# A two-block transformer kernel, rescheduled: new costs and a VectorE/GpSimd exclusion rule in the planner, a late softmax division, and a later write of the embedding

## The chip, the core and the metric

The kernel runs on one core of a Trainium2 chip. The metric is the device time of one execution in microseconds. Before the change it is 3984.7 us, the median of 3 runs (3984.07 to 3984.71).

## The reference, cut to what matters

Two blocks follow each other on 1024 positions of width 1024, all in float32.

- The first block has two layers. Each normalises `x` (and 256 context rows), scales and shifts it by a modulation computed from `c` (`silu(c) @ w_mod + b_mod`), projects it with `w_in`, runs two attentions of 6 heads and a convolution of 31 taps, gates the results and projects them with `w_out`.
- The second block has gated linear attention, a sparse attention of 16 heads over keys that an indexer picks (top 256), a mixing projection, a layer norm, a feed-forward net with a convolution of 3 taps, a layer norm, and a gated embedding (`sigmoid(x @ w_ple_gate) * (p @ w_ple)`) with a last layer norm.

The two places that the change rewrites are these:

```python
h = rms_norm(x, norm_w) * (1.0 + scale[:, None, :]) + shift[:, None, :]   # first layer, modulated input
...
logits = jnp.where(valid[:, :, None, :], logits, -jnp.inf)                # sparse attention
probs = jax.nn.softmax(logits, axis=-1).astype(kv_sel.dtype)
return jnp.einsum('bqhk,bqkc->bqhc', probs, kv_sel)
```

## The kernel before

Activations lie transposed, features on the 128 partitions, positions in chunks `c` of 512 (the context is a chunk of 256). A float32 product is made of three single-pass products: each operand is split into a rounded high part and the rest (`split`: a cast, then a subtraction, `lo`). So nearly every tile costs VectorE, ScalarE or GpSimd two instructions before TensorE may use it.

The program is first written as a list of operations with tags for the stages: `emb` (the products of the embedding), `nm0` (first norm), `mod0` (modulation), `cin0`, `in0`, `conv0`, `mla0`, `gqa0`, `out0` (first layer), the same with 1 (second layer), then `idx`, `score`, `topk`, `gla`, `glap`, `ckv`, `dsa` (sparse attention), `dsap`, `wo2`, `ffn` and `ple`. Each operation names the engines that may run it, with a cost for each (`alts`): sums and differences of two SBUF tiles may go to VectorE (`v`) or GpSimd (`p`), copies to ScalarE (`a`) or VectorE. `Plan.schedule` then walks through a modelled time, picks for each free engine the ready operation of the lowest rank (its place in the list plus `late`), and assigns buffers: 89 pages of 128x512 (`pg`), 8 PSUM banks (`ps`), some small tiles (`sm`). The order that it finds is the order in which each engine's instructions are emitted. So a changed cost changes the order, the engine and the buffers of instructions everywhere.

Every matrix product is recorded at one line (389), every transpose at 393, every sum of two tiles on VectorE at 330 and on GpSimd at 332, every scalar-tensor-tensor at 340, ScalarE's work at 289 and its scalings at 363, VectorE's scalings at 365 and 352. All DMAs are issued by SyncE (403).

In `dsa` a unit is a head and a chunk of 512 queries, four tiles of 128 queries. For each tile: scores (TensorE), masked maximum (line 1796, VectorE), exponentials with their sum (ScalarE), a reciprocal, and a scaling of the probabilities. Then the probabilities are transposed (TensorE), split, and multiplied with the values into the bank `acc`. 32 units run as a pipeline: the scores of the next unit are merged into the products of this one.

At the start `embed` makes 16 tiles in `emb`, and the function `put` (called `early` in `block1`) writes them to DRAM.

## Time and profile before

| | |
|---|---|
| median of 3 runs | 3984.7 us |
| profiled execution | 3984.33 us, of which its span 3982.5 us |
| TensorE busy | 3860.4 us (97%), 18344 matmuls |
| VectorE busy | 3130.6 us (79%) |
| ScalarE busy | 1964.9 us (49%) |
| GpSimd busy | 1520.0 us (38%) |
| mean granted TensorE clock | 0.99 |

TensorE is busy nearly all the time, so what can be had is in the 3%, in the stretches in which its clock is below full, and in what TensorE itself is given to do. A table by stretches of the span is the way to read it, since the idle time is not spread evenly.

### The profile page before, as it was taken

The page shows a single profiled execution, that of the slowest core. Times are in us where ns is not written, and L with a number is a line of the kernel's source. Part 1 is how long each engine was busy: PE and PEld are TensorE (multiplying, and loading weights), DVE is VectorE, ACT ScalarE, POOL GpSimd, SP SyncE. Part 2 cuts the span into 40 slices and gives each one's busy share as a digit, 9 for nine tenths or more (in the row PEclk, how much of TensorE's full clock was granted, in tenths as well). Part 3 has the DMA queues.
Part 4 walks back from the last instruction along what each step waited for, and adds up shares of the span by engine and source line. Part 5 has one row for each costly group of instructions (what it writes and reads, how often), then busy time and mean ns, then how long its engine had stood idle before and what let it go on. Part 6 is the DMA issues. An engine that isn't in the chain of part 4 may idle for free. (4 is left out here: it accounts for less than half of the span.)

```text
span 3982.5 us, 53245 instructions
## 1 busy us (share of the span) xinstructions
PE 3860.4 (97%) x18344; PEld 3100.5 (78%) x18344; DVE 3130.6 (79%) x5241; ACT 1964.9 (49%) x3841; POOL 1520.0 (38%) x1348
## 2 busy tenths in 40 slices
PE   6999999999999999999999999999999999999997
PEld 4778777768878777678988888877778788888876
DVE  8998899996796888857988985788776854446598
ACT  5345577763245566635355731566653432222255
POOL 7654465561252444522354531111143511111177
PEclk8999999999999999999999999999999999999998
DMA  7232222133232110232111332000054411111121
GB/s 247 82 119 79 63 68 65 47 115 135 69 121 72 31 30 20 87 116 73 57 55 60 126 111 77 29 29 34 25 191 127 146 42 49 51 51 43 49 86 57
DMA packets 184975, 311.82 MB, mean 78 GB/s; under 512 B 22912, under 2 KB 46208, under 8 KB 184704
## 3 DMA queue, kind: packets, MB, share of 16 engines
q1 hardware_dynamic: 184704, 308.42, 23.6%
q8 instruction: 144, 2.36, 0.2%
q14 instruction: 127, 1.04, 0.1%
HBM read 237.81 MB, written 62.39 MB: 75 GB/s over the span
## 5 line engine op out<-in xcount | busy, mean ns | idle before, releaser
L389 PE MATMUL ps<-pg,pg 128*128 128x512 f32 (+5 forms) x17008 | 3789.5, 384 | 43.6 <-ACT pg L289 19.8
L389 PEld LDWEIGHTS ps<-pg,pg 128*128 128x128 f32 (+3 forms) x17008 | 2955.4, 188 | 733.5 <-issue 72.9
L332 POOL TENSOR_TENSOR pg<-pg,pg 128x512 fp32r<-128x512 f32 (+4 forms) x1030 | 1437.2, 1411 | 2015.2 <-ACT pg L289 1037.8
L289 ACT ACTIVATE pg<-pg 128x512 fp32r<-128x512 f32 (+7 forms) x1385 | 785.7, 596 | 779.4 <-DVE pg L340 252.1
L289 ACT ACTIVATE pg<-ps 128x512 f32<-128x512 f32 (+10 forms) x1352 | 681.8, 551 | 870.3 <-PE ps L389 708.2
L330 DVE TENSOR_TENSOR pg<-pg,pg 128x512 fp32r<-128x512 f32 (+7 forms) x839 | 769.5, 930 | 150.9 <-ACT pg L289 99.2
L330 DVE TENSOR_TENSOR pg<-ps,pg 128x512 fp32r<-128x512 f32 (+9 forms) x650 | 367.5, 584 | 223.3 <-PE ps L389 133.9
L340 DVE SCALAR_TENSOR_TENSOR pg<-ux,c,pg 128x512 f32<-128x512 f32 x416 | 361.4, 895 | 22.5 <-ACT pg L289 13.9
L373 DVE TENSOR_REDUCE sm<-ps 128x1 f32<-128x512 f32 (+1 forms) x492 | 326.5, 681 | 26.8 <-PE ps L389 23.5
L298 DVE CAST pg<-pg 128x512 fp32r<-128x512 f32 (+4 forms) x342 | 210.9, 623 | 56.2 <-ACT pg L289 24.9
L340 DVE SCALAR_TENSOR_TENSOR pg<-pg,c,pg 128x512 f32<-128x512 f32 (+3 forms) x242 | 223.9, 962 | 5.6 <-ACT pg L289 4.9
L289 ACT ACTIVATE pg<-ps,c 128x512 f32<-128x512 f32 (+1 forms) x182 | 128.0, 708 | 202.9 <-PE ps L389 162.9
L393 PE MATMUL ps<-c,pg 128*128 128x128 f32 (+1 forms) x796 | 163.8, 272 | 11.4 <-DVE pg L298 6.0
L1541 DVE MAX8 sm<-ux 128x8 f32<-128x384 f32 (+5 forms) x192 | 166.9, 884 | 1.3
L1542 DVE MATCH_REPLACE8 ux<-sm,ux 128x384 f32<-128x384 f32 (+5 forms) x192 | 167.4, 875 | 0.0
L298 DVE COPY ux<-ps 128x512 f32<-128x512 f32 x79 | 54.5, 691 | 140.3 <-ACT pg L289 122.6
L389 PE MATMUL ps<-pg,c 128*128 128x512 f32 (+3 forms) x196 | 81.7, 482 | 54.8 <-DVE pg L330 21.7
L393 PEld LDWEIGHTS ps<-c,pg 128*128 128x128 f32 (+1 forms) x796 | 103.9, 141 | 37.9 <-DVE pg L298 6.0
L289 ACT ACTIVATE pg<-pg,sm 128x512 f32<-128x512 f32 (+2 forms) x192 | 116.3, 607 | 18.8 <-DVE sm L352 18.4
L678 ACT ACT_TABLE_LOAD x92 | 118.0, 1283 | 1.6
L383 POOL MEMSET pg<- 128x128 f32 (+2 forms) x193 | 49.9, 274 | 159.7 <-PE ps L389 99.0
L1796 DVE CUSTOM_DVE_ANT_0 pg<-ps,pg 128x512 f32<-128x512 f32 (+3 forms) x176 | 98.8, 573 | 11.6 <-PE ps L389 10.7
(73 smaller groups left out, 1024.7 us busy)
## 6 DMA issues: line engine op xcount, KB each, us to landing
d<-pg SPq DMA_DIRECT2D x202, 256.0 KB, 2.0
pg<-d SPq DMA_DIRECT2D x178, 256.0 KB, 3.5
pg<-in_w2a SPq DMA_DIRECT2D x108, 256.0 KB, 3.0
pg<-in_wmod SPq DMA_DIRECT2D x96, 256.0 KB, 3.3
pg<-in_wup SPq DMA_DIRECT2D x88, 256.0 KB, 2.7
pg<-in_win SPq DMA_DIRECT2D x80, 256.0 KB, 3.4
pg<-in_wout SPq DMA_DIRECT2D x64, 256.0 KB, 3.3
pg<-in_wdn SPq DMA_DIRECT2D x48, 256.0 KB, 2.7
```

The source lines that it names most:

```text
L289: nc.scalar.activation(real(out), real(in_), fn, scale=real(scale), **k)
L298: self.nc.vector.tensor_copy(real(out), real(in_))
L330: self.nc.vector.tensor_tensor(out=real(out), in0=real(in0), in1=real(in1), op=o)
L332: self.nc.gpsimd.tensor_tensor(out=real(out), in0=real(in0), in1=real(in1), op=o)
L340: self.nc.vector.scalar_tensor_tensor(out=real(out), in0=real(in0), scalar=real(scalar), in1=real(in1), op0=o0, op1=o1)
L373: lambda e: self.nc.vector.tensor_reduce(out=real(out), in_=real(in_), axis=AX.X, op=o))
L389: lambda e: self.nc.tensor.matmul(real(out), lhsT=real(lhsT), rhs=real(rhs), start=start, stop=stop))
L393: lambda e: self.nc.tensor.transpose(real(out), real(in_), real(ident)))
L678: nc.scalar.preload_act_table_set(pre)
L1541: P.vec(P.c_v(n), [w], [m8], lambda e, m8=m8, w=w: nc.vector.max(real(m8), real(w)))
L1542: P.vec(P.c_v(n), [w, m8], [w], lambda e, m8=m8, w=w: nc.vector.match_replace(real(w), real(m8), real(w), MARK))
L1796: lambda e, p=p, s=s, n=n, m=mk[t, b], a=sm[:, b:b + 1]: nc.vector.tensor_tensor_reduce(out=real(p), in0=real(s[:, 0:n]), in1=real(m), sca ...
```

## The change

**The planner's costs.** The fixed part of nearly every operation falls: VectorE's sums from 155 to 67 ns, its scalings from 190 to 110, GpSimd's sums from 200 to 92, ScalarE's work from 170 or 202 to 49 or 93. A result is then ready only `TAIL` after its engine is free.

**The exclusion.** Before, an operation on VectorE with SBUF inputs (`dual`) was planned up to 0.42 longer while GpSimd was busy. Now GpSimd's operations and VectorE's `dual` ones are planned one after the other, and GpSimd may take a sum only where VectorE could not have it done sooner.

**The start.** The 16 writes of the embedding (`early()`) are listed behind the modulated inputs. The scaling and shifting of these (`affine`) may go to ScalarE.

**The sparse attention.** The probabilities are no longer scaled. The reciprocals of the four tiles of a unit are transposed onto the feature axis by four transposes of a broadcast column (`rp`), copied to SBUF, and the output is multiplied by them, once for two heads. Maxima, their scaling and the reciprocals are made for four tiles at once; a second block of keys takes the first one's maximum as its start.

```diff
     def c_v(self, n, ex=0):
-        return (n * 1.04 + 155 + ex) / 1000
+        return (n * 1.04 + 67 + ex) / 1000
     def c_p(self, n):
-        return (n * 2.2 + 200) / 1000
+        return (n * 2.2 + 92) / 1000
...
+    def affine(self, out, in_, s, b):
+        def emit(e):
+            if e == "a":
+                self.nc.scalar.activation(real(out), real(in_), AF.Identity, bias=real(b), scale=real(s))
+            else:
+                self.nc.vector.tensor_scalar(out=real(out), in0=real(in_), scalar1=real(s), scalar2=real(b), op0=OP.mult, op1=OP.add)
+        return self.op({"v": (out.n * 0.52 + 110) / 1000, "a": self.c_act(out.n, in_, 93)}, [in_, s, b], [out], emit)
...
+        TAIL = {"t": 0.0, "a": 0.115, "v": 0.083, "p": 0.08, "d": 0.0}
+        hold = {"v": 0.0, "p": 0.0}
...
+                                elif e == "p" and m == "v":
+                                    apart = sum(x.alts["v"] for _, x in ready["v"][:6] if not issued[x.idx] and not x.dual)
+                                    if hold["v"] <= now:
+                                        apart += max(0.0, busy["v"] - now)
+                                    if len(ready["v"]) > 1 and apart + o.alts["v"] < o.alts["p"] + max(0.0, hold["v"] - now):
+                                        ok = False
...
-                    if e == "v" and o.dual and busy["p"] > now:
-                        c += 0.42 * min(busy["p"] - now, c / 0.58)
+                    if e == "p" or e == "v" and o.dual:
+                        other = "p" if e == "v" else "v"
+                        c += max(0.0, hold[other] - now)
+                        hold[e] = now + c
...
-        if c == 1:
-            early()
...
-            P.ts(t, t, a[:, i, k:k + 1].k(2 + k // 4), m[:, i, k:k + 1].k(k // 4), "mult", "add")
+            P.affine(t, t, a[:, i, k:k + 1].k(2 + k // 4), m[:, i, k:k + 1].k(k // 4))
...
+    early()
...
-                    P.ts(sm[:, 2:3], sm[:, 0:1], -(128.0 ** -0.5), None, "mult")
+                P.ts(sm[:, 0, :], sm[:, 0, :], -(128.0 ** -0.5), None, "mult")
...
-                    P.vec(0.08, [sm], [sm], lambda e, sm=sm: nc.vector.reciprocal(real(sm[:, 6:7]), real(sm[:, 4:5])))
-                    for b in range(nb):
-                        P.scale(pn[t, b], pn[t, b], sm[:, 6:7])
+                P.vec(0.2, [sm], [sm], lambda e, sm=sm: nc.vector.reciprocal(real(sm[:, 3, :]), real(sm[:, 1, :])))
...
+                rp = P.ps()
+                for t in range(4):
+                    P.tr(rp[0:64, t * 128:(t + 1) * 128], sm[:, 3, t:t + 1].to_broadcast([128, 64]), ident)
...
+                P.copy(rr[c][G, :].k(i), rp[0:64, :])
...
+                    P.tt(ob[c], ob[c], rr[c], "mult", "vp")
```

GpSimd's queue at the start of the program, before the change: the sums of squares of the first norm (written to one page, pg_220), then the low parts of the modulation weights, 128x512 each.

```order
L332 TENSOR_TENSOR pg_220<-pg_220,pg_227 128x512
L332 TENSOR_TENSOR pg_220<-pg_220,pg_249 128x512
L332 TENSOR_TENSOR pg_220<-pg_220,pg_266 128x512
L332 TENSOR_TENSOR pg_220<-pg_220,pg_276 128x512
L332 TENSOR_TENSOR pg_352<-pg_236,pg_337 128x512
L332 TENSOR_TENSOR pg_373<-pg_246,pg_346 128x512
L332 TENSOR_TENSOR pg_395<-pg_258,pg_377 128x512
L332 TENSOR_TENSOR pg_418<-pg_269,pg_397 128x512
```

The same place in the changed kernel (the sums of squares go to pg_215):

```order
L332 TENSOR_TENSOR pg_215<-pg_215,pg_229 128x512
L332 TENSOR_TENSOR pg_215<-pg_215,pg_256 128x512
L332 TENSOR_TENSOR pg_215<-pg_215,pg_263 128x512
L332 TENSOR_TENSOR pg_363<-pg_241,pg_337 128x512
L332 TENSOR_TENSOR pg_453<-pg_287,pg_416 128x512
L332 TENSOR_TENSOR pg_482<-pg_482,pg_507 128x512
L332 TENSOR_TENSOR pg_203<-pg_203,pg_518 128x512
L332 TENSOR_TENSOR pg_847<-pg_847,pg_853 128x256
```

Of GpSimd's low parts of the modulation weights two are left at this place; the others are now in VectorE's queue. Over the whole program GpSimd's queue goes from 1348 rows to 769, VectorE's from 4932 to 5069, TensorE's from 18083 to 18214.

VectorE's queue in the middle of `dsa` before the change (ISA is the masked maximum and the reading of its result, sm a tile's small numbers):

```order
L1796 ISA pg_26706,sm_26707<-ps_26676,pg_24863 128x512
L1796 ISA sm_26707 128x1
L1807 RECIPROCAL sm_26588<-sm_26588 128x1
L352 TENSOR_SCALAR sm_26660<-sm_26660 128x1
L365 TENSOR_SCALAR pg_26587<-pg_26587,sm_26588 128x128
L1796 ISA pg_26731,sm_26707<-ps_26691,pg_24877 128x128
L1796 ISA sm_26707 128x1
```

And in the changed kernel:

```order
L1824 ISA pg_26641,sm_26608<-ps_26616,pg_24941 128x512
L1824 ISA sm_26608 128x1
L298 COPY pg_26650<-ps_26469 64x512
L1824 ISA pg_26657,sm_26608<-ps_26627,pg_24968,sm_26608 128x384
L1824 ISA sm_26608 128x1
L330 TENSOR_TENSOR pg_26310<-ps_26469,pg_26650 64x512
L330 TENSOR_TENSOR pg_26676<-ps_26634,pg_26663 128x512
L330 TENSOR_TENSOR pg_26684<-ps_26643,pg_26669 128x384
L1835 RECIPROCAL sm_26538<-sm_26538 128x4
```

The scalings of the probabilities are gone, and one reciprocal of 128x4 stands where there were four of 128x1, behind the maxima of all four tiles.

TensorE's queue at the end of a unit of `dsa` in the changed kernel (ps_27351 is the new bank `rp`, c_82 the identity):

```order
L402 MATMUL ps_27342<-pg_27335,pg_25980 64x512
L406 MATMUL ps_27351<-c_82,sm_27154 64x128
L402 MATMUL ps_27342<-pg_27331,pg_26009 128x384
L406 MATMUL ps_27351<-c_82,sm_27154 64x128
L402 MATMUL ps_27342<-pg_27344,pg_26009 64x384
L406 MATMUL ps_27351<-c_82,sm_27154 64x128
L402 MATMUL ps_27342<-pg_27337,pg_26039 128x256
L406 MATMUL ps_27351<-c_82,sm_27154 64x128
```

The four transposes of the reciprocals stand between the last products of the unit, of which the kernel before has only the products.

## Rows read from the trace of the kernel before

**Rows 1.** Stretches of the whole span: busy time of each engine.

```profile
core 0: us, PE busy (x) PEld busy (x) DVE busy (x) ACT busy (x) POOL busy (x), PEclk, DMA share, GB/s
0.00:300.00 300.00, 258.91 (x1217) 201.00 (x1218) 283.69 (x344) 136.11 (x246) 189.97 (x129) 0.94 0.45 149
300.00:1300.00 1000.00, 978.00 (x4541) 765.54 (x4540) 847.00 (x1288) 557.04 (x1042) 441.14 (x394) 1.00 0.26 83
1300.00:2500.00 1200.00, 1192.90 (x5726) 960.89 (x5726) 970.59 (x1594) 619.54 (x1221) 457.77 (x416) 1.00 0.21 70
2500.00:2940.00 440.00, 429.98 (x2342) 350.28 (x2341) 357.57 (x1197) 286.00 (x737) 75.32 (x116) 1.00 0.14 48
2940.00:3200.00 260.00, 255.75 (x1120) 206.63 (x1119) 185.31 (x222) 100.41 (x169) 105.15 (x75) 1.00 0.43 141
3200.00:3800.00 600.00, 599.43 (x2638) 494.04 (x2637) 319.97 (x416) 170.28 (x265) 112.16 (x115) 1.00 0.17 53
3800.00:3982.50 182.50, 145.41 (x772) 122.17 (x770) 166.42 (x185) 95.47 (x166) 138.49 (x103) 0.88 0.18 57
```

**Rows 2.** What TensorE waited for in 0 to 300: total, times, longest.

```profile
PE ps L389 <- ACT pg L289: 16.6, 4, 10.2
PE ps L389 <- POOL pg L332: 7.7, 4, 4.2
```

**Rows 3.** Two stretches of 10 us at the start, columns as in rows 1.

```profile
50.00:60.00 10.00, 4.78 (x11) 1.17 (x10) 9.99 (x19) 3.56 (x7) 8.17 (x6) 0.50 1.06 385
70.00:80.00 10.00, 3.30 (x10) 1.59 (x10) 10.00 (x9) 4.56 (x10) 7.88 (x6) 0.64 0.21 67
```

**Rows 4.** VectorE and GpSimd in order of time, 3806 to 3822: start, length.

```profile
3805.36 0.68 DVE L330 TENSOR_TENSOR pg<-ps,pg 128x512 f32<-128x512 f32 x1
3805.96 4.59 DVE L330 TENSOR_TENSOR pg<-pg,pg 128x512 fp32r<-128x512 f32 x3
...
3805.22 18.41 POOL L332 TENSOR_TENSOR pg<-pg,pg 128x512 f32<-128x512 f32 x11 [0.33 <-ACT pg L289]
```

**Rows 5.** Groups by form, 2300 to 2500; the last row 140 to 150.

```profile
L330 DVE TENSOR_TENSOR pg<-pg,pg 128x512 f32<-128x512 f32 x2 | 1.4, 680 | 0.0
...
L332 POOL TENSOR_TENSOR pg<-pg,pg 128x512 fp32r<-128x512 f32 x32 | 41.4, 1310 | 145.9 <-PE ps L389 76.0 <-ACT pg L289 69.6
...
L340 DVE SCALAR_TENSOR_TENSOR pg<-ux,c,pg 128x512 f32<-128x512 f32 x14 | 9.5, 741 | 0.0
```

**Rows 6.** Groups by form, 0 to 300.

```profile
L340 DVE SCALAR_TENSOR_TENSOR pg<-ux,c,pg 128x512 f32<-128x512 f32 x113 | 98.9, 922 | 0.0
...
L330 DVE TENSOR_TENSOR pg<-pg,pg 128x512 f32<-128x512 f32 x45 | 54.8, 1239 | 0.2
...
L330 DVE TENSOR_TENSOR pg<-pg,pg 128x512 fp32r<-128x512 f32 x29 | 35.2, 1228 | 3.0 <-ACT pg L289 3.0
...
L352 DVE TENSOR_SCALAR pg<-pg,c,c 128x512 f32<-128x512 f32 x16 | 15.1, 985 | 0.0
...
L332 POOL TENSOR_TENSOR pg<-pg,pg 128x512 fp32r<-128x512 f32 x71 | 132.3, 1881 | 77.6 <-ACT pg L289 66.3 <-DVE pg L298 11.1
```

**Rows 7.** TensorE in order of time in dsa; L393 is a transpose.

```profile
2712.86 0.27 PE L393 MATMUL ps<-c,pg 128*128 128x128 f32 x1
2712.89 0.48 PE L389 MATMUL ps<-pg,pg 128*128 128x512 f32 x1
2713.20 0.27 PE L393 MATMUL ps<-c,pg 128*128 128x128 f32 x1
```

**Rows 8.** Groups in dsa, 2490 to 2940.

```profile
L289 ACT ACTIVATE pg<-pg,sm 128x512 f32<-128x512 f32 (+2 forms) x191 | 115.6, 607 | 18.8 <-DVE sm L352 18.4
...
L365 DVE TENSOR_SCALAR pg<-pg,sm 128x512 f32<-128x512 f32 (+3 forms) x91 | 48.8, 542 | 0.5
```

**Rows 9.** What TensorE waited for in 3800 to 3982.5.

```profile
PE ps L389 <- DVE pg L330: 15.6, 2, 10.7
PE ps L389 <- POOL pg L332: 11.5, 2, 8.3
```

More of the change, by code (lines that the diff above doesn't have):

```diff
@@ L266, in c_act @@
     def c_act(self, n, src, extra=0):
-        return (n * 0.836 + (170 if isinstance(src, View) and src.psum else 202) + extra) / 1000
+        return (n * 0.836 + (49 if isinstance(src, View) and src.psum else 93) + extra) / 1000
     def act(self, out, in_, func, bias=None, scale=1.0, accum=None, alts=None):
@@ L277, in act @@
         if accum is not None:
-            ex += 127
+            ex += 92
         fn = getattr(AF, func)
@@ L305, in copy @@
         if "v" in engs:
-            a["v"] = (n * (1.04 if in_.psum else 0.52) + 155) / 1000
+            a["v"] = (n * (1.04 if in_.psum else 0.52) + 70) / 1000
         if "a" in engs:
@@ L352, in emit @@
             self.nc.vector.tensor_scalar(out=real(out), in0=real(in0), scalar1=real(s1), scalar2=real(s2), op0=o0, **k)
-        return self.op({"v": (out.n * (1.04 if in0.psum or accum is not None else 0.52) + 190 + (127 if accum is not None else 0)) / 1000},
+        return self.op({"v": (out.n * (1.04 if in0.psum or accum is not None else 0.52) + 110 + (90 if accum is not None else 0)) / 1000},
                        [in0, s1, s2], [out, accum], emit)
@@ L365, in emit @@
                 self.nc.vector.tensor_scalar(out=real(out), in0=real(in_), scalar1=real(col), scalar2=None, op0=OP.mult)
-        return self.op({"v": (n * (1.04 if in_.psum else 0.52) + 190) / 1000, "a": self.c_act(n, in_, 93)},
+        return self.op({"v": (n * (1.04 if in_.psum else 0.52) + 110) / 1000, "a": self.c_act(n, in_, 93)},
                        [in_, col], [out], emit)
+    def affine(self, out, in_, s, b):
[5 more added lines that the diff above has]
+        return self.op({"v": (out.n * 0.52 + 110) / 1000, "a": self.c_act(out.n, in_, 93)}, [in_, s, b], [out], emit)
     def red(self, out, in_, op="max"):
         o = getattr(OP, op)
-        return self.op({"v": self.c_v(in_.n)}, [in_], [out],
+        return self.vec(self.c_v(in_.n), [in_], [out],
                        lambda e: self.nc.vector.tensor_reduce(out=real(out), in_=real(in_), axis=AX.X, op=o))
     def vec(self, cost, reads, writes, emit):
-        return self.op({"v": cost}, reads, writes, emit)
+        o = self.op({"v": cost}, reads, writes, emit)
+        o.dual = False
+        return o
     def memset(self, ap, val, engs="p"):
@@ L381, in memset @@
         for e in engs:
-            a[e] = (ap.n * (0.85 if e == "p" else 0.52) + 100) / 1000
+            a[e] = (ap.n * (0.85 if e == "p" else 0.52) + 35) / 1000
         return self.op(a, [], [ap], lambda e: self._e(e).memset(real(ap), val))
@@ L596, in schedule @@
                         busy[e] = now + c
-                        fin = now + c
+                        fin = now + c + TAIL[e]
                         stat[e] += c
@@ L1757, in block2 @@
     for hp in range(8):
-        ob = {}
+        ob, rr = {}, {}
         cut = P.side()
@@ L1784, in block2 @@
                 pn = {}
+                G, H = slice(64 * i, 64 * i + 64), slice(64 - 64 * i, 128 - 64 * i)
+                sm = P.buf("sm", (128, 4, 4), F32)
+                nb = 1 + c
                 for t in range(4 * c, 4 * c + 4):
                     qs = slice((t % 4) * 128, (t % 4) * 128 + 128)
-                    sm = P.buf("sm", (128, 4, 4), F32).rearrange("p a b -> p (a b)")
-                    nb = 1 if t < 4 else 2
+                    top = sm[:, 0, t % 4:t % 4 + 1]
                     for b in range(nb):
@@ L1794, in block2 @@
                         p = P.pg()[:, 0:n]
-                        P.vec((n * 1.04 + 200) / 1000, [s, mk[t, b]], [p, sm[:, b:b + 1]],
-                              lambda e, p=p, s=s, n=n, m=mk[t, b], a=sm[:, b:b + 1]: nc.vector.tensor_tensor_reduce(
-                                  out=real(p), in0=real(s[:, 0:n]), in1=real(m), scale=1.0, scalar=BIG, op0=OP.add,
-                                  op1=OP.max, accum_out=real(a)))
+                        first = [top.k(t)] if b else []
+                        P.vec((n * 1.04 + 200) / 1000, [s, mk[t, b]] + first, [p, top.k(t)],
+                              lambda e, p=p, s=s, n=n, m=mk[t, b], a=top, b=b: nc.vector.tensor_tensor_reduce(
+                                  out=real(p), in0=real(s[:, 0:n]), in1=real(m), scale=1.0, scalar=real(a) if b else BIG,
+                                  op0=OP.add, op1=OP.max, accum_out=real(a)))
                         pn[t, b] = p
-                    if nb == 2:
-                        P.tt(sm[:, 0:1], sm[:, 0:1], sm[:, 1:2], "max")
-                    P.ts(sm[:, 2:3], sm[:, 0:1], -(128.0 ** -0.5), None, "mult")
+                P.ts(sm[:, 0, :], sm[:, 0, :], -(128.0 ** -0.5), None, "mult")
+                for t in range(4 * c, 4 * c + 4):
                     for b in range(nb):
-                        P.act(pn[t, b], pn[t, b], "Exp", bias=sm[:, 2:3], scale=128.0 ** -0.5, accum=sm[:, 4 + b:5 + b])
-                    if nb == 2:
-                        P.tt(sm[:, 4:5], sm[:, 4:5], sm[:, 5:6], "add")
-                    P.vec(0.08, [sm], [sm], lambda e, sm=sm: nc.vector.reciprocal(real(sm[:, 6:7]), real(sm[:, 4:5])))
-                    for b in range(nb):
-                        P.scale(pn[t, b], pn[t, b], sm[:, 6:7])
+                        P.act(pn[t, b], pn[t, b], "Exp", bias=sm[:, 0, t % 4:t % 4 + 1].k("e"), scale=128.0 ** -0.5,
+                              accum=sm[:, 1 + b, t % 4:t % 4 + 1].k((t, b)))
+                if nb == 2:
+                    P.tt(sm[:, 1, :], sm[:, 1, :], sm[:, 2, :], "add")
+                P.vec(0.2, [sm], [sm], lambda e, sm=sm: nc.vector.reciprocal(real(sm[:, 3, :]), real(sm[:, 1, :])))
                 lead = P.take(cut)
@@ L1831, in block2 @@
                 P.side()
-                G, H = slice(64 * i, 64 * i + 64), slice(64 - 64 * i, 128 - 64 * i)
+                rp = P.ps()
+                for t in range(4):
+                    P.tr(rp[0:64, t * 128:(t + 1) * 128], sm[:, 3, t:t + 1].to_broadcast([128, 64]), ident)
                 if i == 0:
-                    ob[c] = P.pg()
+                    ob[c], rr[c] = P.pg(), P.pg()
+                P.copy(rr[c][G, :].k(i), rp[0:64, :])
                 t = P.pg()
```

## The prediction

> **What bounds the kernel now.** I read the stretches first [rows 1]: each row has a stretch's length and TensorE's busy time in it, and the difference is TensorE's idle time. From the top: 41.1 us idle in 0 to 300, 22.0 in 300 to 1300, 7.1 in 1300 to 2500, 10.0 in the sparse attention (2500 to 2940), 4.3 in 2940 to 3200, 0.6 in 3200 to 3800, 37.1 in the last 182.5 us: 122 us together. In between TensorE is the bound: 2638 matmuls in 600 us is 0.227 us each. Both ends also run at a granted clock of 0.94 and 0.88 of full speed, that is 36 and 44 us at the lower level (1.2 GHz), after TensorE had been idle. So there are two places to win, the start and the end, and one to lose, whatever TensorE gets to do in addition.
>
> At the start TensorE waits 10.2 us for its very first operand, and after that for GpSimd, ScalarE and VectorE in turn [rows 2]. VectorE is busy 283.7 of 300 us [rows 1], but look at what it does: nine to nineteen instructions in 10 us [rows 3]. The two queues side by side show why: GpSimd runs 11 sums back to back from 3805.2, 1.67 us each [rows 4]. VectorE's sum with a PSUM operand takes 0.68 us beside it, and the next starts 0.60 us after it; three sums with two SBUF operands take 4.59 us. Where GpSimd does little, such a sum takes 0.68 us, and one on GpSimd 1.31 [rows 5]. So the two engines take turns on such operations: 1.67 us for a pair, of which VectorE's part is 0.60. In 0 to 300 VectorE's sums average 1.24 and 1.23 us and its scalar-tensor-tensors 0.92 instead of 0.74 [rows 6].
>
> **The start.** In the order of both programs, of the 145 GpSimd sums in the stages emb, nm0, mod0, cin0, in0 and conv0 24 are left. GpSimd has 129 instructions in this stretch [rows 1], some 115 of them sums, so about 96 leave. On VectorE they cost at most 96 x 0.60 = 58 us, about 53 since some are half as wide. VectorE gets back its stretched time: 45 x (1.239 - 0.680) = 25 us, 29 x (1.228 - 0.680) = 16, 113 x (0.922 - 0.741) = 20 [rows 5, 6], together 61. 17 of the 24 scalings (11 of the wide sort at 0.985, which is 11 us [rows 6]) move to ScalarE, busy 136 of 300. VectorE then needs 283.7 + 53 - 61 - 11 = 265 of 300 us, 35 fewer. TensorE needs 258.9, less up to 18 if it never falls to the lower clock, plus the 10.2 before its first product: 251. So at most 35 us can go, and nothing if TensorE is really late for data. The later writes of the embedding belong here: in SyncE's queue the 16 writes stand between the 18th and the 21st of the 32 loads of modulation weights, and come behind the 26th. That is 4.2 MB that no longer stands ahead of eight loads, while the DMA engines are full (share 1.06, 385 GB/s [rows 3]), some 11 us at that rate. At 70 to 80 the DMA share is 0.21 while VectorE is still full: there it is the two engines, not the transfers. I take -27, near the upper end, since VectorE is the one that is full in both rows.
>
> **First attention, second layer (300 to 1300).** 22 us idle. GpSimd's relief helps where layers begin; but in mla0 and gqa0 89 sums move to VectorE, which already works 847 of 1000 us. I take -4, between -15 (most of the idle time) and +15 (VectorE full, below).
>
> **1300 to 2500, 2940 to 3800.** 7.1 us idle, then 4.9. I take 0 and -3, with bounds of -4 to +8 and -4 to 0.
>
> **The sparse attention.** TensorE gets 128 more transposes (32 units x 4). Where a transpose stands between wide matmuls, one follows another after 0.34 us [rows 7], and the matmul between them is 0.227: 0.11 us for a transpose. 128 x 0.11 = +14 us on the engine that is the bound; nothing hides that. VectorE and ScalarE lose the scalings of the probabilities (192, of which VectorE's 91 take 48.8 us [rows 8]) and three quarters of the small instructions on columns, and get 32 copies and 16 products of a bank's size. VectorE was busy 357.6 of 440 and TensorE's 10 us of idle time follow on short chains, so I take back 6: +8, between +4 (all idle time gone) and +14.
>
> The Trainium skill ("TensorE: Matmul & The Clock Gate", Part 4: PE-mode transpose) gives about 275 ns for one 128x128 transpose within a kernel, and speaks against this part. By it the new ones would cost 128 x 0.275 = 35 us, and the forecast would be 21 us later. The trace has 0.27 us as the length of a transpose too, but 0.11 as its cost between others, since the next matmul starts meanwhile [rows 7]; the row decides.
>
> **The end.** 37.1 us idle, 10.7 of it the last layer norm behind the last product [rows 9], which stays. 26 are left, and up to 22 (half of 44) from the clock, part of it in the tail. In ple GpSimd's sums fall from 67 to 17, and the order of ffn's last part loses some too: some 75 of the 103 GpSimd instructions of this stretch. A wide one that was in turn with VectorE costs the pair 1.67, on VectorE 0.60 + 0.60, so 0.47 less, about half for the half-wide ones: about 27 us of chain. I take -20, between -5 and -32.
>
> **Sum.** -27 - 4 + 0 + 8 - 3 - 20 = -46. The span goes from 3982.5 to 3936.5. The profiled execution takes 1.8 us beyond its span (3984.3), 0.4 us under the median shown, so **3938 us**.
>
> **The rivals.** Time can be told from no change here beyond about 0.2%, 8 us.
>
> - *VectorE becomes the bound in the attentions.* It takes over 89 sums in mla0 and gqa0 (53 us) and 35 in gla. There is room for that on average (153 us in 300 to 1300 [rows 1]), but the heads' softmax is not spread evenly. If half of the 53 us shows up as waits of TensorE, the time is 3938 + 27 = 3965. Chance 0.12.
> - *The start is bound by transfers.* At 50 to 60 the DMA engines are full. If only the 11 us of the moved writes are gained there, the time is 3938 + 16 = 3954. Chance 0.10.
> - *Slower: a unit of the sparse attention waits for its last tile.* Now all exponentials of a unit need the scaled maxima of all four tiles. Behind the last score product come a maximum, a small scaling, and four or eight exponentials of 0.61 us [rows 8]. The new order has 4.2 to 8.0 us of products (at 0.227 us each) between a unit's last score and its first transpose, which needs one exponential, or about 2 us; the fourth transpose of a long unit needs the seventh, or 5 us. If TensorE waited for the whole row, 16 x 4.9 + 16 x 2.4 = 117 us: 4055; for half, 3997. It decides from (46 + 8) / 32 = 1.7 us a unit. Against it: products of the next heads lie between. Chance 0.09.
> - *The exclusion costs nothing.* If the stretched instructions on VectorE only fill time that it has, the ends keep their idle time, and only the transposes stay: 3984 - 4 + 8 - 3 = 3985. That TensorE waits for exactly these engines at both ends [rows 2, 9] speaks against it. Chance 0.03.
> - *The forecast*, between 3905 and 3965. Chance 0.66.
>
> Faster by over 0.2% (under 3976.7): the forecast, the transfers, and two thirds of the first rival, 0.66 + 0.10 + 0.08 = 0.84. Within: its other third and the fourth, 0.07. Slower: 0.09. All lower bounds added (-35, -15, -4, +4, -4, -32) give 3898, the upper ones of three stretches at once (-11 at the start, +15 in the attentions, +14 in dsa, with -3 and -20) 3979. The range is 3900 to 3979; it leaves out the slower rival and the fourth.
>
> **What would show it.** GpSimd's busy time falls from 1520 to about 700 us, and VectorE's sums on two SBUF tiles at both ends go from 1.2 us to near 0.7. In the first 300 us TensorE's busy time rises from 259 to above 275, at a clock near 1.00; in the last 182.5 us its idle time falls below 25. In the sparse attention TensorE's busy time is 14 us more, with fewer than 10 us idle. I am wrong if TensorE's idle time in 0 to 300 stays, if mla0 and gqa0 have idle time that names VectorE, or if the units of the sparse attention start with a wait for ScalarE.

## The result, and the profile after

The changed kernel takes 3920.05 us (median of 4 runs, 3919.01 to 3923.44) beside 3984.70 for the kernel before on the same chip: ratio 0.9836, 95% interval 0.9825 to 0.9848. That is 65 us faster, 18 us below the forecast of 3938. The profiled execution has a span of 3921.6 us.

The stretches of the changed kernel, columns as in [rows 1]; the last one is shorter, since the program ends 61 us earlier:

```profile
0.00:300.00 300.00, 280.29 (x1372) 221.91 (x1373) 280.78 (x506) 160.35 (x287) 23.93 (x28) 0.98 0.48 163
300.00:1300.00 1000.00, 984.21 (x4530) 764.62 (x4528) 817.50 (x1392) 584.36 (x1107) 196.84 (x235) 1.00 0.25 80
1300.00:2500.00 1200.00, 1185.99 (x5717) 957.97 (x5716) 974.14 (x1685) 617.05 (x1241) 276.62 (x270) 1.00 0.21 70
2500.00:2940.00 440.00, 440.00 (x2471) 360.96 (x2470) 311.18 (x816) 250.71 (x652) 70.49 (x112) 1.00 0.19 65
2940.00:3200.00 260.00, 259.39 (x1137) 212.96 (x1136) 175.54 (x256) 101.16 (x166) 34.35 (x31) 1.00 0.34 114
3800.00:3921.60 121.60, 102.54 (x620) 90.46 (x618) 110.13 (x210) 75.33 (x134) 35.40 (x20) 0.93 0.18 59
```

In the first 300 us TensorE is busy 280.3 us instead of 258.9, GpSimd 23.9 instead of 190. In 2500 to 2940 TensorE has no idle time left; in 1300 to 2500 it has 14.0 us instead of 7.1. VectorE's groups by form in 0 to 300, to be held beside [rows 6]:

```profile
L340 DVE SCALAR_TENSOR_TENSOR pg<-ux,c,pg 128x512 f32<-128x512 f32 x120 | 84.0, 742 | 0.1
L330 DVE TENSOR_TENSOR pg<-pg,pg 128x512 fp32r<-128x512 f32 x104 | 71.6, 716 | 4.4 <-ACT pg L289 4.3
L330 DVE TENSOR_TENSOR pg<-pg,pg 128x512 f32<-128x512 f32 x64 | 43.4, 707 | 4.3 <-ACT pg L289 2.1 <-DMA pg<-pg 1.2 <-POOL pg L332 0.9
...
L298 DVE CAST pg<-pg 128x512 fp32r<-128x512 f32 x21 | 9.1, 439 | 0.3
```

VectorE now does 168 sums of this width in 115.0 us (71.6 + 43.4); before it did 74 in 90.0. A sum takes 0.71 us instead of 1.23. So 94 sums more cost it 25 us, not 64.

What TensorE waited for in 0 to 300 and, last row, from 3800 on, beside [rows 2, 9]:

```profile
PE ps L402 <- ACT pg L289: 11.0, 3, 9.2
PE ps L402 <- DVE pg L330: 6.8, 4, 4.2
...
PE ps L402 <- POOL pg L332: 8.6, 1, 8.6
```

Of the waits at the start the first operand's 9.2 us and 6.8 us for VectorE's sums are left, and little else; GpSimd is not named there any more. At the end one wait of size is left, the last layer norm.

**Where the time went.** Stretches of the clock hold different work in two kernels. So I lined the kernels up by TensorE's progress: each matmul of the trace counts by its columns (0.227 us for 512, 0.111 for a 128-column transpose, the new transposes not at all), and a mark is the time at which a kernel has begun the same amount. The kernel before passes the marks at the times of the head row; below stands how many microseconds earlier (+) or later (-) the others pass them, always in the profiled execution. That of the changed kernel is the slowest of its four, 3.4 us above their median. e4 and e6 run the changed kernel's own instructions up to 2440.9 and still differ from its row by up to 2.2 us at the first mark and 3.8 at 2440.9; smaller differences between rows are not told apart.

| mark of before (us) | 369.7 | 946.9 | 1378.8 | 2440.9 | 2969.8 | 3177.4 | 3778.9 | span 3982.5 |
|---|---|---|---|---|---|---|---|---|
| changed kernel | 31.2 | 27.7 | 35.6 | 24.2 | 29.1 | 34.4 | 35.3 | 60.9 |
| e1_no_exclusion | -22.1 | -44.9 | -58.3 | -101.8 | -99.1 | -99.1 | -100.0 | -101.0 |
| e2_before_sums_on_v | 31.6 | 32.5 | 29.6 | 29.8 | 27.7 | 29.4 | 29.5 | 55.6 |
| e3_before_exclusion | 9.4 | -7.9 | 6.5 | 3.1 | -4.5 | 1.6 | 2.4 | 15.7 |
| e9_old_costs | 18.6 | 1.3 | 15.5 | 11.3 | 14.5 | 20.4 | 21.3 | 34.5 |
| e4_after_old_dsa | 33.4 | 28.2 | 38.2 | 28.0 | 42.2 | 48.0 | 48.8 | 74.4 |
| e5_before_new_dsa | -1.1 | -1.5 | -1.1 | -1.1 | 1.7 | 1.8 | 1.8 | 1.8 |
| e6_transposes_twice | 32.1 | 27.1 | 36.9 | 25.5 | 14.8 | 20.0 | 20.9 | 46.6 |
| e7_old_start | 25.1 | 21.2 | 31.4 | 19.2 | 23.3 | 28.5 | 29.4 | 55.1 |
| e8_no_affine | 30.5 | 25.5 | 35.3 | 23.5 | 27.3 | 32.6 | 33.4 | 59.0 |
| e12_sums_more | 29.9 | 30.1 | 42.4 | 42.5 | 40.7 | 42.4 | 42.4 | 68.6 |
| e13_by_stage | 30.2 | 30.1 | 43.0 | 43.1 | 56.8 | 62.6 | 63.4 | 89.0 |
| e14_attention_sums | 30.4 | 10.1 | 20.5 | 11.1 | 24.2 | 30.1 | 30.9 | 56.4 |

A row is read by its differences. The changed kernel gains 31 us up to the first mark (the start), loses 3.5 in the first layer's attentions, gains 8 where the second layer starts, loses 11 up to 2440.9, gains 5 in the sparse attention and 5 behind it, and 26 at the end. Of the 31, 22 are idle time of TensorE up to this mark (42.0 us before, 19.7 after), of the 26, 18 (37.1 and 19.1); the rest is TensorE's busy time, at a granted clock that rises from 0.95 to 0.98 and from 0.90 to 0.96.

### The profile page after: what moved, and what is told of

The parts are those of the page before. It is cut to its first block, busy times and chain, and to the rows that moved or that the text cites. A ratio compares the mean times of both kernels' runs of the same rounds, so it can differ in the third digit from the quotient of the medians.

```text
span 3921.6 us, 52665 instructions
## 1 busy us (share of the span) xinstructions
PE 3852.4 (98%) x18472; PEld 3103.3 (79%) x18472; DVE 3014.1 (77%) x5343; ACT 1967.7 (50%) x3863; POOL 702.2 (18%) x770
## 4 chain that ended last, share of the span: by engine, by line
PE 75%; DVE 8%; ACT 2%; issue 1%; DMA 1%; POOL 0%; SPq 0%; ACTq 0%; DVEq 0%; POOLq 0%
PE ps L402 72%; DVE pg L330 4%; PE ps L406 3%; ACT pg L289 2%; DVE sm L384 1%; DVE pg L340 1%; DVE sm L1565 0%; DVE pg L298 0%; DVE ux L1566 0%; ACT L703 0%; DMA ux<-d 0%; DMA pg<-in_wout 0%; DVE pg L1641 0%; DVE sm L298 0%; DMA pg<-in_win 0%
## 5 line engine op out<-in xcount | busy, mean ns | idle before, releaser
L402 PE MATMUL ps<-pg,pg 128*128 128x512 f32 (+3 forms) x17008 | 3802.6, 385 | 36.1 <-ACT pg L289 14.4
L402 PEld LDWEIGHTS ps<-pg,pg 128*128 128x128 f32 (+2 forms) x17008 | 2945.8, 188 | 714.2 <-issue 69.5
L330 DVE TENSOR_TENSOR pg<-pg,pg 128x512 fp32r<-128x512 f32 (+8 forms) x1420 | 970.9, 708 | 166.9 <-ACT pg L289 113.9
L332 POOL TENSOR_TENSOR pg<-pg,pg 128x512 fp32r<-128x512 f32 (+5 forms) x465 | 627.0, 1355 | 2535.1 <-ACT pg L289 1380.6
L384 DVE TENSOR_REDUCE sm<-ps 128x1 f32<-128x512 f32 (+1 forms) x492 | 325.7, 680 | 21.7 <-PE ps L402 19.2
L340 DVE SCALAR_TENSOR_TENSOR pg<-ux,c,pg 128x512 f32<-128x512 f32 x416 | 318.9, 791 | 18.1 <-ACT pg L289 11.5
L298 DVE CAST pg<-pg 128x512 fp32r<-128x512 f32 (+4 forms) x265 | 127.3, 486 | 88.5 <-ACT pg L289 45.8
L340 DVE SCALAR_TENSOR_TENSOR pg<-pg,c,pg 128x512 f32<-128x512 f32 (+3 forms) x242 | 168.4, 731 | 6.5 <-ACT pg L289 6.0
L298 DVE COPY ux<-ps 128x512 f32<-128x512 f32 x82 | 56.4, 688 | 148.2 <-ACT pg L289 130.8
L1565 DVE MAX8 sm<-ux 128x8 f32<-128x896 f32 (+5 forms) x192 | 167.4, 883 | 2.8 <-DMA ux<-d 0.9
L1566 DVE MATCH_REPLACE8 ux<-sm,ux 128x896 f32<-128x896 f32 (+5 forms) x192 | 167.3, 873 | 0.0
L289 ACT ACTIVATE pg<-pg,sm 128x512 f32<-128x512 f32 (+1 forms) x192 | 115.6, 605 | 29.3 <-DVE sm L352 29.0
L402 PE MATMUL ps<-pg,c 128*128 128x512 f32 (+3 forms) x196 | 74.5, 456 | 20.9 <-POOL pg L332 10.6
L340 DVE SCALAR_TENSOR_TENSOR pg<-ps,c,pg 128x512 f32<-128x512 f32 (+1 forms) x66 | 46.2, 706 | 58.1 <-PE ps L402 54.4
```

Source lines behind the costliest of these rows:

```text
L289: nc.scalar.activation(real(out), real(in_), fn, scale=real(scale), **k)
L298: self.nc.vector.tensor_copy(real(out), real(in_))
L330: self.nc.vector.tensor_tensor(out=real(out), in0=real(in0), in1=real(in1), op=o)
L332: self.nc.gpsimd.tensor_tensor(out=real(out), in0=real(in0), in1=real(in1), op=o)
L340: self.nc.vector.scalar_tensor_tensor(out=real(out), in0=real(in0), scalar=real(scalar), in1=real(in1), op0=o0, op1=o1)
L384: lambda e: self.nc.vector.tensor_reduce(out=real(out), in_=real(in_), axis=AX.X, op=o))
```

## The experiments

Theory: VectorE and GpSimd take turns on sums of SBUF tiles, and the gain at both ends is VectorE's time that GpSimd's sums no longer take. Rivals: the new costs and the order that they give; the edits of the start; the new sparse attention.

### Exclusion, costs, or simply the engine of the sums

**e1_no_exclusion**: the changed kernel without the rule. The new costs stay, and so do the new start, the new sparse attention and a smaller edit (reductions and some other VectorE operations no longer count as `dual`).

```diff
-                                elif e == "p" and m == "v":
-                                    apart = sum(x.alts["v"] for _, x in ready["v"][:6] if not issued[x.idx] and not x.dual)
...
-                    if e == "p" or e == "v" and o.dual:
-                        other = "p" if e == "v" else "v"
-                        c += max(0.0, hold[other] - now)
-                        hold[e] = now + c
+                    if e == "v" and o.dual and busy["p"] > now:
+                        c += 0.42 * min(busy["p"] - now, c / 0.58)
```

> The changed kernel without the exclusion: VectorE's sums may again be planned beside GpSimd, as before, and GpSimd may take any sum; the new costs, the start and the new sparse attention stay. GpSimd's queue goes from 769 rows to 1208. Theory (the gain at both ends comes from GpSimd's sums no longer holding up VectorE's): most of the 31 us at the start and the 25 at the end are lost, so 3960 to 3980 us, and VectorE's sums of two SBUF tiles go back to about 0.9 us on average. Rival (the new costs and the changed order do it, not the exclusion): 3920 within 8 us.

Measured: 4082.89 us, ratio to before 1.0239 (1.0222 to 1.0256). Not 3960 to 3980: 98 us slower than the kernel before, 163 slower than the changed one. VectorE in 0 to 300, then its sums over the whole program with shortest, median and longest time in ns:

```profile
L330 DVE TENSOR_TENSOR pg<-pg,pg 128x512 fp32r<-128x512 f32 x44 | 49.5, 1139 | 5.1 <-ACT pg L289 5.0
...
L330 DVE TENSOR_TENSOR pg<-pg,pg x980: 274/692/2650, 4.7 to 4075.1; 128x512 fp32r<-128x512 f32 x91, 128x512 f32<-128x512 f32 x47, 128x256 fp32r<-128x256 f32 x17, 128x256 f32<-128x256 f32 x13
...
L330 DVE TENSOR_TENSOR pg<-ps,pg x650: 257/680/697, 184.7 to 3958.1; 128x512 fp32r<-128x512 f32 x37, 64x512 f32<-64x512 f32 x28, 128x512 f32<-128x512 f32 x28, 128x128 fp32r<-128x128 f32 x17
```

The stretched sums are back (1.14 us), as the theory has it, and they are those with two SBUF operands alone: none of the 650 with a PSUM operand takes longer than 0.697 us. The size was not foreseen. Over the whole program the stretch is no worse than before (mean of all shapes 883 ns, before 930; of the 128x512 ones alone 941, before 977), and the loss lies in the middle as well (-22 to -102 in the table). What TensorE waited for over the whole of this run:

```profile
PE ps L402 <- DVE pg L298: 46.7, 24, 8.9
PE ps L402 <- DVE pg L330: 39.5, 23, 8.7
PE ps L402 <- ACT pg L289: 37.0, 24, 8.6
PE ps L402 <- POOL pg L332: 20.6, 19, 4.7
```

VectorE's copies and sums and ScalarE's work are late, GpSimd's sums less so. So the new costs, without the rule that goes with them, do harm. The start and the sparse attention, which stay in this run, are not the cause: alone or taken out they move the time by less than 10 us (e5, e7). The smaller edit was not tested alone.

**e2_before_sums_on_v**: the kernel before, its order untouched; where the order puts a GpSimd sum of the named stages, VectorE does it.

```diff
+            if e == "p" and "v" in o.alts and o.tag in ("emb", "nm0", "mod0", "cin0", "in0", "conv0", "ffn", "ple"):
+                e = "v"
             o.emit(e)
```

> The kernel before in its own order and with its own buffers, but the sums that GpSimd does in the stages emb, nm0, mod0, cin0, in0, conv0, ffn and ple are done by VectorE, at the place in its queue at which GpSimd would have started them. GpSimd's queue goes from 1348 rows to 1002; nothing is reordered. Theory (taking turns on SBUF sums is what costs): a sum then costs VectorE 0.68 us and frees it of being held up 0.60 and more, so about 25 us less at the start and 15 to 20 at the end: 3940 us, between 3930 and 3955. Rival (a better order is what gains, the lock alone little): 3984 within 8 us. Rival (VectorE cannot take them): above 3992.

Measured: 3929.24 us, ratio 0.9861 (0.9846 to 0.9876), 56 us faster than before, just past the near end of the 3930 to 3955 expected. No cost, no rule, no reordering, no new start: two lines give 31.6 us at the start and 26 at the end, and nothing between, where nothing was moved. Its stretches:

```profile
0.00:300.00 300.00, 280.56 (x1376) 224.36 (x1377) 275.65 (x514) 148.04 (x265) 0.60 (x12) 0.97 0.47 156
300.00:1300.00 1000.00, 976.39 (x4503) 761.10 (x4502) 838.62 (x1308) 564.79 (x1061) 416.12 (x382) 1.00 0.26 82
```

VectorE works less in the first 300 us than before (275.7 beside 283.7) although it does all of GpSimd's sums (0.6 us of GpSimd left), and TensorE 280.6 beside 258.9. This is the plainest proof of the theory here. One rival stays beside it: a moved sum is also ready sooner, since it takes 0.68 us on VectorE instead of 1.31 to 1.88 on GpSimd [rows 5, 6]. TensorE's waits that name GpSimd were 7.7 us at the start and 11.5 at the end [rows 2, 9]. So at the start that is at most the smaller part of the 31.6; at the end it could be up to 11.5 of the 26, and no run separates the two.

**e3_before_exclusion**: the kernel before with the exclusion (the lines above, the other way round). **e9_old_costs**: the changed kernel with the old fixed costs and no `TAIL`.

```diff
-        return (n * 1.04 + 67 + ex) / 1000
+        return (n * 1.04 + 155 + ex) / 1000
-        return (n * 2.2 + 92) / 1000
+        return (n * 2.2 + 200) / 1000
...
-        TAIL = {"t": 0.0, "a": 0.115, "v": 0.083, "p": 0.08, "d": 0.0}
+        TAIL = {"t": 0.0, "a": 0.0, "v": 0.0, "p": 0.0, "d": 0.0}
```

> The kernel before with only the exclusion in its planner: old costs, old sparse attention, old start. GpSimd's queue goes from 1348 rows to 906. Theory: the exclusion alone gives the start and the end, 27 to 31 and 20 to 25 us: 3930 to 3940 us. Rival (it needs the new costs, since with the old ones a sum on GpSimd still seems cheap): above 3960. If the new sparse attention is what gains in the middle, this run stays some 5 us above the changed kernel beyond what the costs explain.

> The changed kernel with the old fixed costs and without the later readiness of results; exclusion, start and sparse attention as changed. GpSimd's queue has 902 rows instead of 769. Theory (exclusion is the main part): 3920 to 3940 us. Rival (the costs are the main part): above 3955.

Measured: e3 3969.30 us, 0.9960 (0.9945 to 0.9974); e9 3949.15, 0.9911 (0.9897 to 0.9926). Neither is what the theory said. e3 lies above 3960, as its rival had it (the rule needs the new costs); e9 lies between its theory (up to 3940) and its rival (above 3955). e3 is 24 us ahead where the kernel before is at 261 us (the changed kernel 27), and falls back to 9 by the first mark. TensorE's waits in its stretch 230 to 370:

```profile
PE ps L391 <- DVE pg L330: 11.7, 4, 5.9
PE ps L391 <- ACT pg L289: 2.4, 3, 0.9
```

There GpSimd is nearly idle (8.6 us of 140) and TensorE waits for VectorE's sums: with the old costs the rule seems to give VectorE its work in an order in which these come late (argued from these waits; no run changes that order alone). So rule and costs need each other: the costs are worth 29 us where the rule is (e9 to the changed kernel), the rule 163 where the costs are (e1), and e2 needs neither for the two ends.

### The sparse attention

**e4_after_old_dsa** has the changed planner and start with the sparse attention of before, **e5_before_new_dsa** the other way round, **e6_transposes_twice** is the changed kernel with each new transpose issued twice.

```diff
     def tr(self, out, in_, ident, twice=1):
+        def emit(e):
+            for _ in range(twice):
+                self.nc.tensor.transpose(real(out), real(in_), real(ident))
...
-                    P.tr(rp[0:64, t * 128:(t + 1) * 128], sm[:, 3, t:t + 1].to_broadcast([128, 64]), ident)
+                    P.tr(rp[0:64, t * 128:(t + 1) * 128], sm[:, 3, t:t + 1].to_broadcast([128, 64]), ident, 2)
```

> The changed kernel with the sparse attention of before (the probabilities scaled, no transposes of the reciprocals: 128 transposes fewer on TensorE). By the prediction's term (+8 us) it is 8 us faster, 3912 us. By the two traces (the stretch from the first product of the sparse attention to its last gained 5 us in spite of the transposes, since TensorE's idle time went to zero) it is about 5 us slower, 3925 us. If the idle time went away for another reason (the costs, the exclusion), 14 us faster: 3906.

> The kernel before with the new sparse attention alone. The prediction's term says +8 us (3993); the two traces say -5 us (3980), with TensorE's idle time in the sparse attention at or near zero. If the gain there comes from the costs or the exclusion, it is +14 us (3999).

> The changed kernel in its own order, but each of the 128 transposes of a broadcast reciprocal is issued twice in a row, with the same operands (256 instead of 128). If one costs TensorE 0.11 us, the time rises by 14 us, to 3934; if it costs the 0.27 us that an instruction's length shows, by 35 us, to 3955; if they cost nothing, because they lie in time in which TensorE waits anyway, within 4 us of 3920. Half the columns (64 instead of 128) could halve the 0.11: then +7.

Measured: e4 3910.68 us, 0.9814 (0.9800 to 0.9827), 9 us faster than the changed kernel; e5 3981.99, 0.9992 (0.9983 to 1.0000), 3 us faster than before, within what can be told; e6 3937.47, 0.9880 (0.9865 to 0.9895), 17 us slower than the changed kernel. So the price of this edit depends on the plan around it. In the kernel before it costs nothing (e5, near the 3980 of my reading of the two traces, and not the 3993 of the prediction's term); in the changed kernel it costs 9 us, near the prediction's +8, and there my reading was the wrong one: it put down to the edit what the planner did. Two stretches of e4 in the sparse attention, and then of e5:

```profile
2500.00:2600.00 100.00, 99.65 (x554) 82.05 (x553) 80.85 (x285) 68.98 (x179) 11.18 (x21) 1.00 0.09 29
2600.00:2700.00 100.00, 99.65 (x554) 82.15 (x554) 82.31 (x283) 68.51 (x176) 11.05 (x23) 1.00 0.10 34
```

```profile
2500.00:2600.00 100.00, 100.00 (x569) 83.05 (x568) 67.80 (x193) 55.48 (x150) 13.19 (x22) 1.00 0.07 23
2600.00:2700.00 100.00, 100.00 (x571) 82.60 (x570) 70.57 (x189) 53.76 (x142) 16.99 (x26) 1.00 0.10 34
```

With the old sparse attention and the changed planner TensorE is idle 0.35 us in 100, without the new transposes. With the new sparse attention and the old planner it is not idle at all, and VectorE works some 70 us of 100 instead of the 81 and 82 in e4. So each of the two alone takes most of the idle time away. From the mark 2440.9 to 2969.8 the kernel before takes 528.9 us, e5 526.1, the changed kernel 524.0 and e4 514.7. Where TensorE has idle time (10.5 us in this stretch before, 0.9 in e5), the edit takes it back and costs nothing; where it has little (2.5 us in e4, 0 in the changed kernel), the edit costs 9.3 us. Issued twice, the transposes cost 15.5 us more in this stretch, 0.12 us each (17.4 / 128 = 0.14 by the medians).

### The start

**e7_old_start** undoes both edits of the start, **e8_no_affine** only the scaling on ScalarE.

```diff
-            P.affine(t, t, a[:, i, k:k + 1].k(2 + k // 4), m[:, i, k:k + 1].k(k // 4))
+            P.ts(t, t, a[:, i, k:k + 1].k(2 + k // 4), m[:, i, k:k + 1].k(k // 4), "mult", "add")
...
+        if c == 1:
+            early()
...
-    early()
```

> The changed kernel with the old start: the 16 writes of the embedding are listed where they were, between the loads of the modulation weights, and the modulated inputs are scaled by VectorE alone. Theory (VectorE freed of GpSimd is the whole gain at the start; the kernel before with sums moved to VectorE gained 31 us there without either edit): within 4 us of 3920. Rival, as the prediction's working had it in part (11 us of scalings leave VectorE, 11 us of writes leave the way of the loads): 3930 to 3942.

> The changed kernel with the modulated inputs scaled by VectorE alone; the late writes of the embedding stay. The old start as a whole (both edits undone) cost 8.8 us. If the scalings are what counts there (VectorE is the bound at the start), this run is 6 to 9 us above the changed kernel, 3926 to 3929; if the writes of the embedding are, within 3 us of 3920; if both count, 3923 to 3925.

Measured: e7 3928.80 us, 0.9857 (0.9844 to 0.9871); e8 3924.93, 0.9847 (0.9833 to 0.9860), an interval that overlaps that of the changed kernel. My theory of "within 4 us" fell for e7, which is 9 us above the changed kernel, just short of the rival's 3930. e8's median is 4.9 us above, where its expectation had "both count". But at the first mark e8 is 0.7 us behind the changed kernel and e7 6.1. So at the start the writes of the embedding count for some 5 us, and the scalings for less than rows of the same start differ by (2.2); where the rest of e8's difference lies, if it is one, the traces do not tell. In e7 TensorE waits for ScalarE's work 14.9 us in 0 to 300 instead of 11.0. But e2 reaches 31.6 us with both old edits and another order, so this is worth something only in the order that the changed planner makes; why is open.

### How far it reaches

**e12_sums_more** is e2 with mod1, cin1, in1 and conv1 (nm1 has no such sum) added to the list of stages. **e13_by_stage** takes this list without ffn and ple, the old costs and order up to the sparse attention, and from there on the new ones, with the old sparse attention and the old start. **e14_attention_sums** adds the four attentions to e13's list.

```diff
+NEW = ("dsa", "dsap", "wo2", "ffn", "ple")
...
-        return (n * 1.04 + 67 + ex) / 1000
+        return (n * 1.04 + (67 if self.new() else 155) + ex) / 1000
...
-                                elif e == "p" and m == "v":
+                                elif e == "p" and m == "v" and o.tag in NEW:
...
+            if e == "p" and "v" in o.alts and o.tag in ("emb", "nm0", "mod0", "cin0", "in0", "conv0", "nm1", "mod1", "cin1", "in1", "conv1"):
+                e = "v"
```

> The kernel before in its own order, with the sums of the first layer's start and of the end on VectorE (that run took 3929) and now also those of mod1, cin1, in1 and conv1, the start of the second layer: 72 GpSimd instructions fewer again. If taking turns with GpSimd is what TensorE waits for there too, as at the start, it regains the 8 us that the changed kernel gained at this place: 3921. Rival (what the changed kernel gained there was only the waits of the first attention given back, or a better order): 3929 within 4 us.

> A version put together from the parts that gained: up to the sparse attention the order of the kernel before with the sums of both layers' starts on VectorE, no change at the start otherwise; from the sparse attention on the new costs and the exclusion, with the old sparse attention (no transposes of reciprocals). By stretches as measured against the kernel before: start 31, second layer's start 8 (if it is the same mechanism; else 0), middle 0, sparse attention 14, the stretch behind it 6, end 26: 85 us together, 3900 (3908 without the 8). Rival (the gain in the sparse attention depends on what the planner did ahead of it): 3914 to 3922.

> The version put together by stage (3896 us), with the sums that GpSimd still does in the four attentions of the layers (mla0, gqa0, mla1, gqa1; 310 GpSimd instructions) done by VectorE as well, in place. Theory, with its limit: a sum moved costs VectorE 0.68 us, and only those that were in turn with a sum of VectorE give some 0.60 back; where VectorE is the fuller engine, moving stops to pay. In the first layer's attentions VectorE works some 85 to 90 of 100 us, of which about 13 are time that GpSimd's sums take from it; 181 sums in some 480 us add 123 us and give at most 65 back, so it would work 97 of 100 or more and TensorE would wait for it there: 10 to 40 us slower than 3896. Rival (GpSimd is not worth using anywhere: every sum moved gains, as at the start): 3880 to 3896.

Measured: e12 3914.77 us, 0.9821 (0.9808 to 0.9835); e13 3896.13, 0.9774 (0.9761 to 0.9787); e14 3927.82, 0.9855 (0.9838 to 0.9871). e12 gains 14 us over e2, nearly all where the second layer starts (from 30.1 to 42.4 in the table): the same mechanism there, larger than the 8 that the changed kernel got. e13 was put together from stretches and expected at 3900. It is 24 us faster than the changed kernel, the fastest here. Three of its stretches:

```profile
300.00:1300.00 1000.00, 987.48 (x4564) 773.09 (x4563) 840.68 (x1399) 571.36 (x1071) 303.41 (x317) 1.00 0.26 82
1300.00:2500.00 1200.00, 1193.84 (x5788) 966.95 (x5788) 971.45 (x1668) 624.28 (x1250) 446.68 (x404) 1.00 0.21 70
2500.00:2940.00 440.00, 437.16 (x2361) 359.38 (x2360) 350.57 (x1127) 281.43 (x693) 60.12 (x101) 1.00 0.20 68
```

In 1300 to 2500 GpSimd is as busy as before the change (447 us beside 458), TensorE's idle time is 6.2 us instead of the changed kernel's 14.0, and in the sparse attention it is 2.8 us, without the transposes. e14 shows the limit: it is 32 us slower than e13, within the 10 to 40 expected. The stretch 480 to 840, the first layer's attentions, in e13 and then in e14:

```profile
480.00:840.00 360.00, 356.72 (x1592) 263.41 (x1590) 342.57 (x552) 265.20 (x515) 197.43 (x182) 1.00 0.24 71
```

```profile
480.00:840.00 360.00, 347.89 (x1523) 249.45 (x1521) 351.70 (x662) 254.78 (x496) 14.62 (x37) 1.00 0.22 66
```

With GpSimd's 197 us gone, VectorE is busy 351.7 of 360 us (97.7%) and TensorE falls from 356.7 to 347.9. By the mark 946.9 e14 has lost 20 us to e13, by 2440.9 32 us, the whole of the difference. Here GpSimd earns its place.

## Why the prediction was right, and where a step failed

**The mechanism was right.** That the two engines take turns, 1.67 us for a pair of which 0.60 are VectorE's own, was read from [rows 4 to 6], and e2 shows on its own that VectorE gets back more than the moved sums cost it. The Trainium skill ("SBUF — State Buffer", section "Who interferes with whom") says that a VectorE instruction with two SBUF inputs contends with a GpSimd instruction that reads SBUF, and that one with a single SBUF input does so only in a two-port mode, which casts and scalings can enter. The 650 sums with a PSUM operand, none above 0.697 us, agree, and so do the casts and scalings below.

**Term by term**, predicted for the stretches and measured between the marks, which lie at most 80 us from the stretches' bounds:

| stretch | predicted | measured | |
|---|---|---|---|
| start | -27 | -31.2 | right, within the bound of -35 |
| to 1378.8 | -4 (-15 to +15) | -4.4 | right in sum; its parts, -8 at the second layer's start and +3.5 in the attentions, had no size in the forecast |
| to 2440.9 | 0 (-4 to +8) | +11.4 | loss put at nothing, outside its bounds |
| sparse attention | +8 (+4 to +14) | -4.9 | wrong sign for the stretch |
| behind it, to 3778.9 | -3 (-4 to 0) | -6.2 | right way, but twice the size and outside its bounds |
| end | -20 | -25.6 | right, within -5 to -32 |
| sum | -46 | -60.9 | -64.7 by the medians |

The total came out within its range partly by luck: the sparse attention missed by 13 us to one side and the stretch 1300 to 2500 by 11 to the other.

*The sparse attention* is the step that failed. The term was 14 us for the transposes ("nothing hides that"), less 6 of idle time. In the kernel before, from whose rows it was worked out, the edit alone (e5) raises TensorE's busy time in this stretch by 6.8 us, not 14, and takes back 9.6 us of idle time, not 6: 2.8 us faster. And what the changed planner does there stood at nothing: with the old sparse attention it gives back 14 us (e4, 528.9 to 514.7). Costs and rule do that together: the rule with the old costs (e3) loses 7.6 us in this stretch, and no run has the new costs alone there. That the edit then costs 9 us on top of the new plan, near the +8, is luck: it is 11.8 us of busy time less 2.5 of idle time. I looked for what the edit adds and did not ask what a new plan does to a stage whose instructions are many and short.

The 0.11 us for a transpose is borne out roughly: 0.12 to 0.14 when doubled, 0.07 to 0.09 when taken out (9.3 and 11.8 us over 128). The Trainium skill ("TensorE: Matmul & The Clock Gate", Part 4: PE-mode transpose) has about 275 ns for one, for bf16 and within one kernel; by it, as an estimate, e6 would have been 35 us slower. It was 17, so here the measurement decides.

*1300 to 2500* loses 11.4 us, 8 of them between 1827 and 1929 us of the kernel before. Every kernel planned throughout with the exclusion loses 7 to 8 us there (the changed one, e3, e4, e6, e7, e8, e9), none without it does (e1, e2, e5, e12, e13, e14). Most of the rest, 5 us, falls between 2137 and 2341. In the changed kernel, 1840 to 1880, and then the kernel before, 1860 to 1880:

```profile
1840.00:1860.00 20.00, 16.79 (x76) 13.61 (x74) 20.00 (x34) 13.92 (x27) 7.12 (x2) 1.00 0.20 70
1860.00:1880.00 20.00, 18.07 (x88) 15.55 (x89) 19.18 (x38) 6.25 (x14) 7.79 (x7) 0.83 0.36 119
```

```profile
1860.00:1880.00 20.00, 20.00 (x100) 17.13 (x99) 20.00 (x43) 20.00 (x49) 0.00 (x0) 1.00 0.31 111
```

In the changed kernel VectorE is busy the whole of the first 20 us, TensorE waits once, 5.1 us, for a sum of VectorE, and its granted clock is then lower for a while (0.83 in the next 20 us). VectorE is full in the kernel before too, without a wait; but over the stretch it works 88.5 us there and 96.9 in the changed kernel, with 16 wide sums of SBUF tiles instead of 5. This looks like the first rival, VectorE as the bound, at a place where I had not priced it; no run moves these sums alone.

*The start* had its size right for a reason that was partly wrong. The bound of 35 us is 300 less VectorE's 265; of it 16 us are time in which VectorE did nothing before either, and only 19 what it saves, 11 of these by the scalings moved to ScalarE. They are worth 0.7 us at the start by the traces (e8, within their noise), and a scaling takes 0.54 us once GpSimd is out of the way, not the 0.985 of [rows 6]. The 11 us for the moved writes came out at about 5 (e7 less e8).

*The rivals.* VectorE as the bound in the attentions came true in part: the changed kernel moved 89 sums there and lost 6 us between 481 and 831 us of the kernel before, where I had 27; e14, which moves all, loses 32 to e13 over both layers. The start bound by transfers is refuted by e2, which gains 31.6 us there with the writes of the embedding where they were. The waits of a sparse attention unit for its last tile did not come: TensorE's idle time there is zero. That VectorE's held-up time costs nothing is refuted by e2.

**The marks of the prediction.** GpSimd is busy 702 us (about 700 foreseen), VectorE's wide sums average 0.71 us at the start and 0.71 and 0.77 (two forms) from 3700 on, TensorE is busy 280 in 300 us, its last 182.5 us have 19.1 us of idle time (below 25). The clock at the start is 0.98. In the sparse attention TensorE's busy time is 10 us more in 440 (14 foreseen), with no idle time. One of the signs of being wrong came in small: from 480 to 840, in the first layer's attentions, TensorE is idle 7.5 us instead of 4.2, and 5.0 us of its waits name VectorE (2.4 before).

**What stays open:** why the new costs without the rule lose 98 us. VectorE's wide sum was planned at 0.69 us and is now planned at 0.60 (512 x 1.04 + 67 ns), ready 0.08 later (`TAIL`); in e1 it measures 0.94 on average, so the plan may promise VectorE's results earlier than they come, and TensorE waits for its copies and sums. That this is the cause is argued, not shown: no run changes the costs alone.

## What to carry to other kernels

Look at the time of one instruction form in two places of the same trace before counting busy time: a VectorE at 95% whose sums take 1.23 us here and 0.68 there is not full, it is held up, and taking work from the engine beside it makes it faster although it then does that work itself. Such a shift pays until the engine is full with its own lone times, so it is decided stage by stage, and the parts that gained can be put together stage by stage, with their gains added up. A planner's costs and the rule that corrects them belong together: the rule alone was worth 16 us (e3), the costs without the rule did harm (e1), and an edit inside a stage has to be priced against the stage as the new plan leaves it.

## What the runs showed of the hardware that was not expected

- Not only sums with two SBUF operands are held up by GpSimd. VectorE's casts from SBUF to SBUF take 439 ns in the first 300 us of the changed kernel and 928 in e1 (with the order left as it was: 780 before, 420 in e2); its scalings with two columns take 540 ns in e2 and 985 before [rows 6]. That is a factor of 2.1 and 1.8, no less than for the sums (1.23 to 0.71).
- The new transposes write 64 partitions instead of 128, with 128 columns each as before (the "half the columns" of e6's expectation are these partitions). Doubled, they are not cheaper for it: 0.12 to 0.14 us each, beside the 0.11 of [rows 7].
